# Routing and gathering the first 128 tokens during the second 128's Fourier map, with the norm's weights moved into the router and tiles placed 128 bytes over multiples of 256

## The chip, the cores and the metric

The kernel runs on one core of one Trainium2 chip. The metric is the device time of one execution in microseconds (us); the runs of the kernel before gave a median of 1440.93 us. TensorE is called PE here (PEld is its loading of stationary operands), VectorE is DVE, ScalarE is ACT, GpSimd is POOL and SyncE is SP.

## What is computed

A two-layer encoder on 256 tokens of width 1024, all in float32. Layer 0 is a retention mixer and a dense SwiGLU; layer 1 is a 2-D Fourier mixer with a linear map and a top-2-of-8 expert SwiGLU. The part that the change touches:

```python
h = h + fourier_mixer(rms_norm(h, mix_norm[1]), fnet_w_out)     # real part of a 2-D FFT, then @ w_out
t = rms_norm(h, ffn_norm[1])
logits = t @ w_router                                           # 256 x 8
top_val, top_idx = lax.top_k(logits, 2)
gates = sum(one_hot(top_idx) * softmax(top_val)[..., None])
for e in range(8):
    out = out + gates[:, e:e+1] * ((silu(t @ w_gate[e]) * (t @ w_up[e])) @ w_down[e])
h = rms_norm(h + out, final_norm)
```

Each expert has w_gate and w_up of 1024 x 3584 and w_down of 3584 x 1024.

## The kernel before

The 256 tokens are two chunks of 128, called c = 0 and 1. Every float32 operand is split into a high part, rounded to float32r by ACT (L252, weights L130), and the remainder, by DVE (L253, weights L131); a product is three matmuls (hi*hi, lo*hi, hi*lo: L247, L248, L249). Weights come as 1 MB tiles `raw` over SP's DMA queue (L104), in the order of use, into slots that are given out as soon as a tile is split; the split tiles `whi` and `wlo` have three buffers. Late in the program four more slots are lent (L905 to L909); the first of them, `y`, lies where the pool `pt` of the Fourier stage lay.

The order of work on each engine is the order in which the program is written (a manual schedule); engines meet by semaphores.

`close` (L318) ends a stage that adds to the residual X: for each of the four quarters (chunk c, half hf of the width) it does twelve 512-column matmuls, then `gained` (DVE adds the result into X, L265, and multiplies by the norm's weights into `gx`, L266), and then hands the quarter before to `sink`. For the Fourier map the sink is `r_sink` (L808): PE transposes the gained quarter (L811), ACT copies it to `xt` (L812), the high and low parts `nh`, `nl` are made and the squares are summed (L280). One quarter later the router's matmuls run, 8 columns wide and in plain float32, four of them (8 PE instructions) for each quarter (`r_mm`, L769).

`route(c)` (L774) finds the two largest logits with DVE (L777 to L783) and makes `mask`. `po` counts with PE how many tokens before this one chose each expert (L824 for chunk 0; L827 and L828 for chunk 1), DVE copies it to `pos` (L826, L829). `gates` (L785) works the weights of the two experts out on POOL.

For experts 0 and 1, `choose` (L839) makes one-hot matrices `pm` from pos and mask (L844, one for each chunk and expert), `gather` (L848) picks the tokens with 256-column matmuls (L854 with `nh`, L855 with `nl`; eight for each of four pairs of 128 columns, 32 in all), and the result is split into `xe`. `place` transposes `pm` (L866) and picks the gates (L871). In the kernel before, all this comes after both chunks are routed, and `place` comes in the middle of the first expert's first product, after one weight tile. Each weight tile of an expert is twelve 512-column matmuls; an expert has 7 blocks of six tiles.

`Aligned` places every tile of 512 bytes or more at a multiple of `ALIGN` bytes from the start of its pool. The pools begin 128 bytes over a multiple of 256 (X lies at byte 1152 of each partition), except `pt`, which is filled so that it begins at a multiple of 256. With steps of 128, tiles lie at either. The program's own addresses are: `whi`, `wlo`, `raw`, `nhi`, `nlo`, `th`, `yh`, `yl` and the experts' `hth`, `htl` 128 over a multiple of 256; the dense SwiGLU's `hth`, `htl` (178944, 183040 and on) and `tdh`, `tdl` at multiples of 256. The dense `hth` and `htl` are stationary operands of the down product, as `yh` and `yl` are of the Fourier map and the experts' `hth` and `htl` of theirs, all with `whi` or `wlo` as the moving operand.

Of the kernel before, what the change touches and what calls it, by code (L numbers as in the profile page):

```python
# [12 lines left out]
OP = mybir.AluOpType  # L13
# [8 lines left out]
NE = 8  # L22
# [18 lines left out]
class Aligned:  # L41


    ALIGN = 128

    def __init__(self, pool):
        self.pool, self.at, self.seen = pool, 0, set()
# [104 lines left out]
def body(nc, tc, a, out, upto=None):  # L152
    with ExitStack() as ctx:
# [75 lines left out]

        def route_consts(rw):  # L230
            nc.scalar.dma_start(rw, a["moe_router"][0].rearrange("(k p) e -> p k e", p=P))
            kw = dict(base=0, allow_small_or_imprecise_dtypes=True)
            ge.iota(iota8, pattern=[[1, NE]], channel_multiplier=0, **kw)
            ge.iota(slot, pattern=[[1, P]], channel_multiplier=0, **kw)
            ge.memset(ones, 1.0)
# [39 lines left out]
        def sq_tile():  # L275
            return const.tile([P, 2, 2], F32, name="sq", bufs=2)
# [38 lines left out]
                    mm3(accs[2 * c + hf], lh[j][:, cp(c)], ll[j][:, cp(c)], it[0][:, j, HALF[hf]],  # L315
                        it[1][:, j, HALF[hf]], first and j == 0, last and j == 1)

        def close(its, accs, sink, early=None):  # L318

            left = None
            for c in range(2):
                for hf in range(2):
                    for i, (it, lh, ll) in enumerate(its):
                        out_mm(accs, it, lh, ll, c, False, i == len(its) - 1, (hf,))
                    xg = gained(c, hf, accs)
                    if early:
                        early(c, hf)  # L330
                    if left:
                        sink(*left)
                    left = (c, hf, xg)
            return lambda: sink(*left)
# [269 lines left out]
        td = [pt.tile([P, 2, 512], F32R, name=n) for n in ("tdh", "tdl")]  # L604
        ts_ = [pt.tile([P, 2, 2 * H1], F32R, name=n) for n in ("tsh", "tsl")]
        rw = pt.tile([P, 8, NE], F32, name="rw")
        pt.fill(96)
        with tc.tile_pool(name="pb", bufs=1) as pb:
            pb = Aligned(pb)
# [86 lines left out]
        if upto == "B":  # L696
            return finish()


        with tc.tile_pool(name="pc", bufs=1) as pc:  # L700
            pc = Aligned(pc)
# [60 lines left out]

            xt = [pc.tile([P, 8, P], F32, name="xt", tag="fh", bufs=2) for _ in range(2)]
            lgp = [mm("lg") for _ in range(2)]
            sq, late = sq_tile(), []

            def r_mm(c, hf):
                for k in range(4 * hf, 4 * hf + 4):
# [39 lines left out]
            def r_sink(c, hf, xg):  # L808
                p = tr()
                for k in range(4):  # L810
                    te.transpose(p[:, cp(k)], xg[:, cp(k)], ident)  # L811
                se.copy(xt[c][:, 4 * hf:4 * hf + 4], p.rearrange("p (k t) -> p k t", k=4))  # L812
                for ch in late:
                    r_mm(*ch)
                late[:] = [(c, hf)]
                split(nh[:, c, HALF[hf]], nl[:, c, HALF[hf]], xg)
                square(sq, c, hf)

            left = close(its, accs, r_sink)
            po = mm("po")  # L820
            route(0)
            left()
            r_mm(1, 1)
            te.matmul(po[:, 0:8], upper, mask[:, 0], start=True, stop=True)  # L824
            route(1)
            ve.tensor_copy(pos[:, 0], po[:, :8])  # L826
            te.matmul(po[:, 8:16], ones, mask[:, 0], start=True, stop=False)  # L827
            te.matmul(po[:, 8:16], upper, mask[:, 1], start=False, stop=True)  # L828
            ve.tensor_copy(pos[:, 1], po[:, 8:16])  # L829
            gates()  # L830

        pt_.close()
        if upto == "C":
# [2 lines left out]

        with tc.tile_pool(name="pe", bufs=1) as pe:
            pe = Aligned(pe)
            def choose(e0):  # L839

                pm = pe.tile([P, 2, 2 * P], F32R, name="pm")
                for c in range(2):
                    for j in range(2):
                        ve.tensor_scalar(pm[:, c, cp(j)], slot, pos[:, c, e0 + j:e0 + j + 1],  # L844
                                         mask[:, c, e0 + j:e0 + j + 1], op0=OP.is_equal, op1=OP.mult)
                return pm

            def gather(pm, xe, q, o=None):  # L848

                o = o or mm("ga")  # L850
                for i in range(2):
                    ds = cp(2 * q + i)
                    for c in range(2):
                        te.matmul(o[:, i * 256:(i + 1) * 256], nh[:, c, ds], pm[:, c], start=c == 0, stop=False)  # L854
                        te.matmul(o[:, i * 256:(i + 1) * 256], nl[:, c, ds], pm[:, c], start=False, stop=c == 1)  # L855
                ov = o.rearrange("p (i j s) -> p j i s", i=2, j=2)
                split(xe[:, :, 0, 2 * q:2 * q + 2], xe[:, :, 1, 2 * q:2 * q + 2], ov)

            def place(pm):

                pt = pe.tile([P, 2, S], F32R, name="pt", bufs=2)
                gl = pe.tile([P, 2, NE + 1], F32, name="gl", bufs=2)
                p = tr()
                for j in range(2):
                    for c in range(2):
                        te.transpose(p[:, j * S + c * P:j * S + (c + 1) * P], pm[:, c, cp(j)].bitcast(F32), ident)  # L866
                se.copy(pt, p.rearrange("p (j t) -> p j t", j=2))
                p = acc(3)
                for j in range(2):
                    for c in range(2):  # L870
                        te.matmul(p[:, 16 * j:16 * j + NE + 1], pm[:, c, cp(j)].bitcast(F32), gts[:, c],  # L871
                                  start=c == 0, stop=c == 1)
                ve.tensor_copy(gl, p[:, :32].rearrange("p (j e) -> p j e", j=2)[:, :, :NE + 1])
                return pt, gl

            XE, PT, GT, RS = {}, {}, {}, {}

            def prep(e0):

                st = {}  # L880

                def first():
                    st["pm"] = choose(e0)
                    st["xe"] = pe.tile([P, 2, 2, 8, P], F32R, name="xe", bufs=2)
                    for j in range(2):
                        XE[e0 + j] = st["xe"][:, j]
                yield first
                for q in range(4):
                    yield lambda q=q: gather(st["pm"], st["xe"], q, acc(q) if not e0 else None)

                def last():
                    pt, gl = place(st["pm"])
                    for j in range(2):
                        PT[e0 + j] = pt[:, j]
                        GT[e0 + j] = gl[:, j, e0 + j:e0 + j + 1]
                        RS[e0 + j] = gl[:, j, NE:]
                yield last

            work = list(prep(0))
            for f in work[:-1]:  # L900
                f()
            work = work[-1:]

            i0 = W.next
            W.lend(pe.tile([P, 2048], F32, name="lent", tag="y"), i0 + 40)  # L905
# [152 lines left out]
            for u in range(NU):  # L1058
                e, b = divmod(u, 7)
                if b == 0 and e % 2 == 1 and e + 1 < NE:  # L1060
                    work += list(prep(e + 1))
                if b == 1 and e:
                    work[:0] = [lambda e=e, c=c: add_back(e - 1, c) for c in range(2)]
                if u == OVER_AT + 3:
                    work += [lambda hf=hf: final_gain(hf) for hf in range(2)]
                if u == NU - 5:
                    work += [lambda c=c: final_parts(c) for c in range(2)]
                for s, o in enumerate(moe_h(e)):
                    if s == 0 and u:
                        hidden_t(u - 1)  # L1070
                    if s == 0 and not u:
                        work.pop(0)()
                hm = pe.tile([P, 512], F32, name="hm")
                se.activation(hm, o, AF.Silu, scale=RS[e])
                for s, o in enumerate(moe_h(e)):
                    if s == 0 and work:
                        work.pop(0)()
                ve.scalar_tensor_tensor(hm, o, RS[e], hm, op0=OP.mult, op1=OP.mult)
                hms[u] = hm
                if u == NU - 1:  # L1080
                    final_start(1)
                if u:
                    moe_down(u - 1, (lambda: hidden_t(NU - 1)) if u == NU - 1 else None)
                if work:
                    work.pop(0)()
                if u == NU - 2:
                    final_start(0)
                if u == OVER_AT - 2:
                    counts()
                if u == OVER_AT - 1:  # L1090
                    most = nc.values_load(cmi[0:1, 0:1])
                    tc.mark_branch_hint_location("over", most > P, engines=[te.engine, ve.engine, nc.sync.engine])
                if u == OVER_AT:
                    nc.scalar.dma_start(gb[:1], a["final_norm"].rearrange("(o d) -> o d", o=1))
                    ov = overflow_tiles()
                    with tc.If(most > P, label="over"):  # L1096
                        overflow(**ov)
# [73 lines left out]
```

## Time and profile before

| | before |
|---|---|
| median of 3 runs | 1440.93 us (1440.27 to 1440.96) |
| the profiled execution | 1440.99 us, span 1439.2 us |
| PE busy | 1419.8 us (99%) |
| DVE, ACT, POOL busy | 1184.3, 971.0, 61.4 us |
| closing quarters of the Fourier map | about 426 to 439 us of the span |
| routing, gathering, first expert's first tiles | 439 to 457 us |
| experts | 452.6 to about 1430 us |

A row of the timeline gives start, duration, engine, line, operation, output and inputs, shape and count; a bracket at its end is the engine's idle time before it and what ended it. Matmuls overlap their neighbours, so their rate is read from start to start, not from their durations.

### The profile page before, as it was taken

Reading aid. Unit: us, or ns where it says so; the run is one execution under the profiler, and the core shown is the slowest. Engines: PE = TensorE matmul, PEld = TensorE weight load, DVE = VectorE, ACT = ScalarE, POOL = GpSimd, SP = SyncE. Lnnn points to the kernel's source line nnn. Section 1 sums busy time; section 2 is a strip of 40 time slices with the busy share of each in tenths; the row PEclk is TensorE's granted clock in tenths of the full one; section 3 lists DMA queues with packets and bytes.
Section 4 is the critical chain, followed back from the end, with each engine's and each line's share of the span. In section 5 each row is a group of like instructions: output and inputs, shape, how many; then the busy total and the mean of one; then the engine's idle time right before and its main releaser. Section 6 shows DMA issues by size and latency. Waiting matters only on the chain. (4 is left out here: it accounts for less than half of the span.)

```text
span 1439.2 us, 17455 instructions
## 1 busy us (share of the span) xinstructions
PE 1419.8 (99%) x6603; PEld 1178.0 (82%) x6603; DVE 1184.3 (82%) x1236; ACT 971.0 (67%) x1123; POOL 61.4 (4%) x95
## 2 busy tenths in 40 slices
PE   8999999999999999999999999999999999999997
PEld 6888878888888888888888888888878888888886
DVE  6876666545577999989999998998989899999996
ACT  5544446444456777777777777777777777777875
POOL 8400000000001000000000000000000000000000
PEclk9999999999999999999999999999999999999999
DMA  8646539655536989999999999999999999999980
GB/s 286 213 152 204 189 120 389 232 192 188 176 133 239 392 299 365 346 343 334 374 354 373 377 344 339 366 375 335 348 388 346 340 364 366 374 366 375 355 319 30
DMA packets 185101, 431.70 MB, mean 300 GB/s; under 512 B 7977, under 2 KB 10801, under 8 KB 185010
## 3 DMA queue, kind: packets, MB, share of 16 engines
q1 hardware_dynamic: 181424, 426.27, 82.2%
q10 hardware_dynamic: 3586, 4.24, 0.9%
q8 instruction: 54, 0.88, 0.3%
q14 instruction: 37, 0.30, 0.1%
HBM read 429.44 MB, written 1.05 MB: 299 GB/s over the span
## 5 line engine op out<-in xcount | busy, mean ns | idle before, releaser
L131 DVE TENSOR_TENSOR wlo<-raw,whi 128x1024 fp32r<-128x1024 f32 (+1 forms) x789 | 923.9, 1221 | 141.0 <-ACT whi L130 135.5
L130 ACT CAST whi<-raw 128x1024 fp32r<-128x1024 f32 (+1 forms) x789 | 786.1, 1047 | 200.7 <-PE acc L249 101.4
L247 PE MATMUL mm<-whi,xe 128*128 128x512 f32 x896 | 355.0, 396 | 0.3 <-PEq L1096 0.3
L249 PE MATMUL mm<-whi,xe 128*128 128x512 f32 x896 | 349.6, 390 | 0.0
L248 PE MATMUL mm<-wlo,xe 128*128 128x512 f32 x896 | 349.2, 390 | 0.0
L247 PE MATMUL acc<-whi,hth 128*128 128x512 f32 x528 | 206.2, 390 | 0.0
L249 PE MATMUL acc<-whi,htl 128*128 128x512 f32 x528 | 205.9, 390 | 0.0
L248 PE MATMUL acc<-wlo,hth 128*128 128x512 f32 x528 | 205.9, 390 | 0.0
L249 PEld LDWEIGHTS mm<-whi,xe 128*128 128x128 f32 x896 | 168.2, 188 | 36.0
L247 PEld LDWEIGHTS mm<-whi,xe 128*128 128x128 f32 x896 | 168.3, 188 | 34.9 <-issue 2.2
L248 PEld LDWEIGHTS mm<-wlo,xe 128*128 128x128 f32 x896 | 168.6, 188 | 32.9
L247 PE MATMUL mm<-whi,nhi 128*128 128x512 f32 (+1 forms) x352 | 135.7, 386 | 0.0
L249 PE MATMUL mm<-whi,nlo 128*128 128x512 f32 (+1 forms) x352 | 133.9, 380 | 0.0
L248 PE MATMUL mm<-wlo,nhi 128*128 128x512 f32 (+1 forms) x352 | 133.7, 380 | 0.0
L249 PEld LDWEIGHTS acc<-whi,htl 128*128 128x128 f32 x528 | 99.1, 188 | 21.1
L247 PEld LDWEIGHTS acc<-whi,hth 128*128 128x128 f32 x528 | 99.2, 188 | 20.8
L248 PEld LDWEIGHTS acc<-wlo,hth 128*128 128x128 f32 x528 | 99.2, 188 | 20.8
L252 ACT CAST hth<-tr 128x512 fp32r<-128x512 f32 (+1 forms) x67 | 38.9, 581 | 90.6 <-PE tr L293 90.6
L249 PEld LDWEIGHTS mm<-whi,nlo 128*128 128x128 f32 x352 | 66.2, 188 | 12.9
L248 PEld LDWEIGHTS mm<-wlo,nhi 128*128 128x128 f32 x352 | 66.3, 188 | 12.0
L247 PEld LDWEIGHTS mm<-whi,nhi 128*128 128x128 f32 x352 | 66.2, 188 | 11.8
L253 DVE TENSOR_TENSOR htl<-tr,hth 128x512 fp32r<-128x512 f32 (+1 forms) x67 | 45.8, 683 | 32.7 <-ACT hth L252 32.6
(279 smaller groups left out, 1037.6 us busy)
## 6 DMA issues: line engine op xcount, KB each, us to landing
raw<-in_moe_w_gate SPq DMA_DIRECT2D x110, 1024.0 KB, 7.1
raw<-in_moe_w_down SPq DMA_DIRECT2D x108, 1024.0 KB, 7.0
raw<-in_moe_w_up SPq DMA_DIRECT2D x105, 1024.0 KB, 7.1
raw<-in_ret_w_in SPq DMA_DIRECT2D x23, 1024.0 KB, 5.2
raw<-in_dense_w_gate SPq DMA_DIRECT2D x11, 1024.0 KB, 5.1
raw<-in_dense_w_up SPq DMA_DIRECT2D x11, 1024.0 KB, 8.8
raw<-in_dense_w_down SPq DMA_DIRECT2D x11, 1024.0 KB, 5.8
raw<-in_ret_w_out SPq DMA_DIRECT2D x8, 1024.0 KB, 4.8
```

What stands on the lines that cost most here:

```text
L130: self.nc.scalar.copy(hi[sl], t[sl])
L131: self.nc.vector.tensor_sub(lo[sl], t[sl], hi[sl].bitcast(F32))
L247: te.matmul(o, lh, rh, start=first, stop=False)
L248: te.matmul(o, lh, rl, start=False, stop=False)
L249: te.matmul(o, ll, rh, start=False, stop=last)
L252: se.copy(hi, src)
L253: ve.tensor_sub(lo, src, hi.bitcast(F32))
```

## The change

`ALIGN` becomes 256, so that every large tile lies 128 bytes over a multiple of 256. The norm's weights are loaded as a 128 x 8 tile `rg` and multiplied into the router's weights `rw` on POOL, so that the router can read X itself: the transposes of `r_sink` take X in place of the gained tile. `close` gets a hook `mid`: the sink of the quarter before now comes after the first six matmuls of a quarter, not after all twelve, and in the last quarter the router's matmuls for chunk 0 and `route(0)` come there too. After the quarters, chunk 0's counts, choice and gathering are done while chunk 1's last quarter, its router matmuls and its routing go on; the gathers of chunk 0 start the four accumulators `acc` and those of chunk 1 finish them. `place` comes before the first expert. The choice matrix of experts 0 and 1 lies in the buffer of `tdh` in the pool `pt`.

```diff
 class Aligned:
-    ALIGN = 128
+    ALIGN = 256
...
         def route_consts(rw):
             nc.scalar.dma_start(rw, a["moe_router"][0].rearrange("(k p) e -> p k e", p=P))
+            nc.scalar.dma_start(rg, a["ffn_norm"][1].rearrange("(k p) -> p k", p=P))
+            ge.tensor_mul(rw, rw, rg[:, :, None].to_broadcast([P, 8, NE]))
...
-        def close(its, accs, sink, early=None):
+        def close(its, accs, sink, early=None, mid=None):
...
                     for i, (it, lh, ll) in enumerate(its):
                         out_mm(accs, it, lh, ll, c, False, i == len(its) - 1, (hf,))
+                        if mid and left and not i:
+                            mid(c, hf)
+                            sink(*left)
                     xg = gained(c, hf, accs)
                     if early:
                         early(c, hf)
-                    if left:
+                    if left and not mid:
                         sink(*left)
...
+        def choose(pm, e0, c):
+            for j in range(2):
+                ve.tensor_scalar(pm[:, c, cp(j)], slot, pos[:, c, e0 + j:e0 + j + 1],
+                                 mask[:, c, e0 + j:e0 + j + 1], op0=OP.is_equal, op1=OP.mult)
+
+        def gather(o, pm, q, c):
+            for i in range(2):
+                ds = cp(2 * q + i)
+                te.matmul(o[:, i * 256:(i + 1) * 256], nh[:, c, ds], pm[:, c], start=not c and not i, stop=False)
+                te.matmul(o[:, i * 256:(i + 1) * 256], nl[:, c, ds], pm[:, c], start=False, stop=bool(c and i))
...
             def r_sink(c, hf, xg):
                 p = tr()
                 for k in range(4):
-                    te.transpose(p[:, cp(k)], xg[:, cp(k)], ident)
+                    te.transpose(p[:, cp(k)], X[:, c, cp(4 * hf + k)], ident)
                 se.copy(xt[c][:, 4 * hf:4 * hf + 4], p.rearrange("p (k t) -> p k t", k=4))
-                for ch in late:
-                    r_mm(*ch)
-                late[:] = [(c, hf)]
                 split(nh[:, c, HALF[hf]], nl[:, c, HALF[hf]], xg)
                 square(sq, c, hf)
 
-            left = close(its, accs, r_sink)
-            po = mm("po")
-            route(0)
+            def r_mid(c, hf):
+                if (c, hf) == (1, 1):
+                    r_mm(0, 0)
+                    r_mm(0, 1)
+                    route(0)
+
+            left = close(its, accs, r_sink, mid=r_mid)
+            po, pm = mm("po"), pt.tile([P, 2, 2 * P], F32R, name="pm0", tag="tdh")
+            te.matmul(po[:, 0:8], upper, mask[:, 0], start=True, stop=True)
+            r_mm(1, 0)
+            ve.tensor_copy(pos[:, 0], po[:, :8])
+            choose(pm, 0, 0)
             left()
+            go = [acc(q) for q in range(4)]
+            for q in range(2):
+                gather(go[q], pm, q, 0)
             r_mm(1, 1)
-            te.matmul(po[:, 0:8], upper, mask[:, 0], start=True, stop=True)
             route(1)
-            ve.tensor_copy(pos[:, 0], po[:, :8])
-            te.matmul(po[:, 8:16], ones, mask[:, 0], start=True, stop=False)
-            te.matmul(po[:, 8:16], upper, mask[:, 1], start=False, stop=True)
-            ve.tensor_copy(pos[:, 1], po[:, 8:16])
+            for q in range(2, 4):
+                gather(go[q], pm, q, 0)
+            po = tr()
+            te.matmul(po[:, 0:8], ones, mask[:, 0], start=True, stop=False)
+            te.matmul(po[:, 0:8], upper, mask[:, 1], start=False, stop=True)
+            ve.tensor_copy(pos[:, 1], po[:, :8])
+            choose(pm, 0, 1)
             gates()
+            for q in range(4):
+                gather(go[q], pm, q, 1)
+            ro = place(pm)
...
-            work = list(prep(0))
-            for f in work[:-1]:
+            for f in prep(0, go, ro):
                 f()
-            work = work[-1:]
+            work = []
...
                     if s == 0 and u:
                         hidden_t(u - 1)
-                    if s == 0 and not u:
-                        work.pop(0)()
```

`prep(0, go, ro)` only splits what was gathered (`split_xe`) and copies what `place` left in PSUM (`placed`); for the later pairs of experts `prep` does what it did.

## Rows read from the trace of the kernel before

**Rows 1.** Page, busy time of the engines over the span.
```profile
PE 1419.8 (99%) x6603; PEld 1178.0 (82%) x6603; DVE 1184.3 (82%) x1236; ACT 971.0 (67%) x1123; POOL 61.4 (4%) x95
```

**Rows 2.** Busy time by stretch of the span; the first row names the columns.
```profile
core 0: us, PE busy (x) PEld busy (x) DVE busy (x) ACT busy (x) POOL busy (x), PEclk, DMA share, GB/s
...
439.20:444.10 4.90, 3.90 (x35) 3.75 (x33) 4.30 (x16) 3.45 (x8) 0.57 (x3) 1.00 0.00 0
444.20:450.90 6.70, 5.11 (x23) 5.04 (x24) 2.49 (x10) 0.86 (x2) 4.41 (x15) 0.50 0.55 184
460.00:1400.00 940.00, 939.70 (x4303) 777.85 (x4303) 864.88 (x835) 726.73 (x794) 0.00 (x0) 1.00 0.98 357
```

**Rows 3.** Timeline of PE from the last closing quarter to the first gather.
```profile
439.13 0.60 PE L811 MATMUL tr<-ident,gx 128*128 128x128 f32 x4
...
440.88 0.63 PE L811 MATMUL tr<-ident,gx 128*128 128x128 f32 x4 [0.36 <-ACT nhi L252]
...
441.35 1.90 PE L769 MATMUL lg<-rw,xt 128*128 128x8 f32 x16
...
444.89 0.59 PE L827 MATMUL po<-mask,ones 128*128 128x8 f32 x2 [1.43 <-DVE pos L826]
...
446.81 0.55 PE L854 MATMUL acc<-pm,nhi 128*128 128x256 f32 x1 [0.90 <-DVE pm L844]
```

**Rows 4.** Timeline of DVE, chunk 0's routing, then chunk 1's position and choice.
```profile
441.50 0.16 DVE L777 COPY lgt<-lg 128x8 f32<-128x8 f32 x1
...
442.65 0.23 DVE L783 SCALAR_TENSOR_TENSOR mask<-iota,if,o 128x8 f32<-128x8 f32 x1
...
445.95 0.17 DVE L829 COPY pos<-po 128x8 f32<-128x8 f32 x1 [1.11 <-PE po L828]
446.06 1.11 DVE L844 TENSOR_SCALAR pm<-slot,pos,mask 128x128 fp32r<-128x128 f32 x4
```

**Rows 5.** Timeline of PE: 20th of 32 gathers, first and second expert tiles.
```profile
451.01 0.28 PE L855 MATMUL acc<-pm,nlo 128*128 128x256 f32 x1
...
452.56 0.40 PE L247 MATMUL mm<-whi,xe 128*128 128x512 f32 x1
...
456.56 0.48 PE L247 MATMUL mm<-whi,xe 128*128 128x512 f32 x1
```

**Rows 6.** Timeline of ACT and DVE: the first expert weight tiles split after the gathers.
```profile
453.24 3.89 ACT L130 CAST whi<-raw 128x1024 fp32r<-128x1024 f32 x4
...
454.32 4.63 DVE L131 TENSOR_TENSOR wlo<-raw,whi 128x1024 fp32r<-128x1024 f32 x4 [0.26 <-ACT whi L130]
```

**Rows 7.** Timeline of PE: dense closing (47 matmuls), then the Fourier map (71).
```profile
390.80 0.39 PE L248 MATMUL acc<-wlo,hth 128*128 128x512 f32 x1
...
401.50 0.40 PE L249 MATMUL acc<-whi,htl 128*128 128x512 f32 x1
...
415.75 0.40 PE L248 MATMUL acc<-wlo,yh 128*128 128x512 f32 x1
...
431.63 0.39 PE L249 MATMUL acc<-whi,yl 128*128 128x512 f32 x1
```

**Rows 8.** Groups of PE from 250 to 401.6 us; L248, L249 have x88 each too.
```profile
L247 PE MATMUL acc<-whi,hth 128*128 128x512 f32 x88 | 34.9, 397 | 0.0
```

**Rows 9.** Timeline of DVE: the first closing quarter's result added into X.
```profile
429.98 0.68 DVE L265 TENSOR_TENSOR X<-X,acc 128x512 f32<-128x512 f32 x1
```

**Rows 10.** Waits from 460 to 1400 us: us in total, times, longest.
```profile
SPq L104 <- DVE wlo L131: 774.3, 313, 9.9
...
DVE wlo L131 <- DMA raw<-in_moe_w_down: 1.3, 5, 0.3
```

**Rows 11.** Timeline of SP's queue: the first lent slots.
```profile
446.07 0.92 SPq L104 DMA_DIRECT2D lent<-in_moe_w_up  x2
```

**Rows 12.** Timeline of ACT where the router's weights are loaded.
```profile
226.51 0.45 ACTq L231 DMA_DIRECT2D rw<-in_moe_router  x1
...
236.76 2.00 ACT L130 CAST whi<-raw 128x1024 fp32r<-128x1024 f32 x2 [3.43 <-PE mm L249]
```

More of the change, by code (lines that the diff above doesn't have):

```diff
@@ L606, in body @@
         rw = pt.tile([P, 8, NE], F32, name="rw")
+        rg = pt.tile([P, 8], F32, name="rg")
         pt.fill(96)
@@ L697, in body, with place @@
             return finish()
+        def choose(pm, e0, c):
[7 more added lines that the diff above has]
+                te.matmul(o[:, i * 256:(i + 1) * 256], nl[:, c, ds], pm[:, c], start=False, stop=bool(c and i))
+        def place(pm):
+            p = tr()
+            for j in range(2):
+                for c in range(2):
+                    te.transpose(p[:, j * S + c * P:j * S + (c + 1) * P], pm[:, c, cp(j)].bitcast(F32), ident)
+            g = mm("gl")
+            for j in range(2):
+                for c in range(2):
+                    te.matmul(g[:, 16 * j:16 * j + NE + 1], pm[:, c, cp(j)].bitcast(F32), gts[:, c],
+                              start=c == 0, stop=c == 1)
+            return p, g
         with tc.tile_pool(name="pc", bufs=1) as pc:
@@ L764, in body @@
             lgp = [mm("lg") for _ in range(2)]
-            sq, late = sq_tile(), []
+            sq = sq_tile()
             def r_mm(c, hf):
@@ L838, in body, with split_xe @@
             pe = Aligned(pe)
[L839 to L855, printed above, removed]
+            def split_xe(o, xe, q):
@@ L856, in gather, with placed @@
                 ov = o.rearrange("p (i j s) -> p j i s", i=2, j=2)
                 split(xe[:, :, 0, 2 * q:2 * q + 2], xe[:, :, 1, 2 * q:2 * q + 2], ov)
-            def place(pm):
+            def placed(o):
                 pt = pe.tile([P, 2, S], F32R, name="pt", bufs=2)
                 gl = pe.tile([P, 2, NE + 1], F32, name="gl", bufs=2)
[L863 to L873, printed above, removed]
+                se.copy(pt, o[0].rearrange("p (j t) -> p j t", j=2))
+                ve.tensor_copy(gl, o[1][:, :32].rearrange("p (j e) -> p j e", j=2)[:, :, :NE + 1])
@@ L874, in place, with prep @@
                 return pt, gl
             XE, PT, GT, RS = {}, {}, {}, {}
-            def prep(e0):
+            def prep(e0, go=None, ro=None):
                 st = {}
                 def first():
-                    st["pm"] = choose(e0)
+                    if not go:
+                        st["pm"] = pe.tile([P, 2, 2 * P], F32R, name="pm")
+                        for c in range(2):
+                            choose(st["pm"], e0, c)
                     st["xe"] = pe.tile([P, 2, 2, 8, P], F32R, name="xe", bufs=2)
@@ L887, in prep, with part @@
                 yield first
+                def part(q):
+                    o = go[q] if go else mm("ga")
+                    for c in () if go else range(2):
+                        gather(o, st["pm"], q, c)
+                    split_xe(o, st["xe"], q)
                 for q in range(4):
-                    yield lambda q=q: gather(st["pm"], st["xe"], q, acc(q) if not e0 else None)
+                    yield lambda q=q: part(q)
                 def last():
-                    pt, gl = place(st["pm"])
+                    pt, gl = placed(ro or place(st["pm"]))
                     for j in range(2):
```

## The prediction

> **What bounds the kernel now.** I read the busy times first. PE is busy for 1419.8 of 1439.2 us [rows 1], so only two things can move the end: PE time that is lost around the change, and the rate at which PE's matmuls follow each other. Then the stretches: among the experts PE is busy 939.7 of 940 us at the full clock, while from 439.2 to 450.9 us it is idle for 2.6 us in all, and from 444.2 to 450.9 us the granted clock is 0.50, that is 1.2 instead of 2.4 GHz [rows 2]. So the routing is the soft place. Its timeline shows what PE waits for: 0.36 us for `nhi` before the last transposes, 1.43 us for chunk 0's `pos` (which stands behind chunk 1's routing on DVE), and 0.90 us for the choice [rows 3]. After that PE gathers: 32 matmuls from 446.81 to 452.56 us, the first 19 in 4.20 us, the other 13 in 1.55 us [rows 3, 5], so 221 ns each and then 119 ns each. At the later rate the 32 take 3.81 us; the half clock costs 1.94 us here. Losses before: 0.36 + 1.43 + 0.90 + 1.94 = 4.6 us, without the count matmuls that ran at half clock too.
>
> **The reordering.** The number of PE instructions stays: as many transposes, router matmuls, counts and gathers, and `place` only goes ahead of the first expert tile. So I compare PE's losses. Where it will wait in the new order:
>
> - The sink after six matmuls. The transposes of quarter 0 now need X's sum, which DVE has ready at 429.98 + 0.68 = 430.66 us [rows 9]; six matmuls of the second quarter end their slots at 431.63 - 5 x 0.227 = 430.50 us [rows 7]. 0.2 us; DVE's part of the sink then delays the next sum a little. For the four quarters 0.3 us.
> - Before chunk 0's gathers. After the last matmul (0.39 us till its result) DVE must do the sum, the gained product of the same width (0.68 each), chunk 0's pos (0.17) and two of four choices (0.55) [rows 4, 9]: 2.5 us, and about 0.4 more because `route(0)` and one split stand ahead of the sum on DVE. In that time PE has the counts, eight router instructions (half of 1.90 us) and four transposes (0.63) [rows 3], together with 0.3 for the counts 1.9 us. Without the choice PE stands for 1.0 us; I take 1.3 with the signals.
> - Before chunk 1's counts. `route(1)` takes 441.50 to 442.88 us on chunk 0's rows, 1.38 us [rows 4], and PE has eight gathers (0.95) and the first counts under it. 0.4 us.
> - Before chunk 1's gathers. Counts, pos, choice as now, where that wait was 0.90 us [rows 3]. 1.0 us.
>
> Sum 3.0 us against 4.6 us: a gain of 1.6 us, if PE keeps the full clock. What is late next is the split of the second expert tile. Now it is needed at 456.56 us; its casts begin at 453.24 and the first `wlo` comes 1.16 us (a quarter of 4.63) after 454.32, at 455.48 us [rows 5, 6]. In the new order `place` is done before the experts begin, and PE wants that tile at 456.56 - 1.6 = 455.0 us, while ACT must first copy what `place` left, and its casts begin hardly earlier. That ties; 0 to 0.3 us, I take 0.1. The gain is 1.5 us, between 1.2 and 1.9.
>
> **The clock.** This is what the gain hangs on. Before, the last dense matmuls end and the transposes begin at 439.13 us, and the next dense work is the first gather at 446.81 us: 7.7 us of transposes, 8-column matmuls and waiting, within which the clock fell [rows 2, 3]. In the new order the quarter's last six matmuls come after `route(0)`'s matmuls, and the longest such stretch before the gathers is about 3 us; then come eight gathers, one us without, eight more, and about 2 us without. No row shows what the clock does after a gap of that kind; I take the shorter gaps as a reason to expect 2.4 GHz, at little better than even.
>
> The Trainium skill, "TensorE: Matmul & The Clock Gate", Part 1, speaks against that: the throttled clock is the default state and activity releases it. By that rule thin gathers between waits could leave PE at 1.2 GHz; the trace agrees so far, since the clock fell in just this work. The sum by it is the second rival's.
>
> **The 256-byte steps.** The 47 dense matmuls with `hth` or `htl` as stationary operand take 10.70 us for 46 steps, 232.6 ns each; the 71 with `yh` or `yl` take 15.88 us for 70 steps, 226.9 ns, at the same clock, shape and moving operands [rows 7]. The first tiles lie at a multiple of 256, the second 128 over. There are 3 x 88 = 264 dense ones [rows 8]: 264 x 5.7 ns = 1.5 us. If the place is not the cause, nothing is gained; if the fastest steps seen are reached, some 1.6. I take 1.5, as it is the only difference that the listing of the tiles shows, and as PE does not wait there. `whi`, `wlo` and `raw` keep their place, so the experts' rate stays.
>
> **The norm in the router.** One more load from ACT's queue and a product on POOL. The load of `rw` takes 0.45 us to issue [rows 12]; if ACT also waits for a semaphore of an older load, the idle 3.43 us before 236.76 us [rows 12] takes that up. POOL is busy 61.4 us in all [rows 1], and the product is needed 200 us later. Nothing; without that cover at most 3.4 us of PE waiting, which the end would see.
>
> **Transfers.** The first lent slot `y` reaches into the pool `pt`. Now it is issued at 446.07 us [rows 11]; in the new order `pm0` lies in `pt` until `place` has read it, at about 452.3 us, and everything behind it in SP's queue waits, four lent loads and the refills. 6.2 us later at most. The cover is the lead of the loads: among the experts the queue waits 774 us for free slots, and DVE waits 1.3 us for weights [rows 10]. With 15 slots of 2.72 us each (twelve matmuls), weights are there tens of us ahead. I take nothing.
>
> **Sum.** The profiled execution took 1440.99 us, 0.06 above the median of the runs. 1440.99 - 1.5 - 1.5 = 1438.0 us.
>
> **The rivals.**
>
> - Clock holds, both gains come: 1438.0 us, from 1437.0 to 1438.8 by the bounds above. Chance 0.50.
> - The clock falls as before and returns as before, at about 451 us. Then half of chunk 0's gathers, the router's and count matmuls and the first of chunk 1's gathers run at half clock: some 16 gathers x 0.1 us and 0.3 for the rest, 1.9 us, mostly on the chain, which eats the routing's gain. 1439.6 us. For it: the thin work; against it: the shorter gaps. Chance 0.20.
> - The same, but gathers in two thin groups do not bring the clock back before the experts: chunk 1's 13 other gathers 1.3 us more and `place` about as much again. 1441 to 1442 us. Chance 0.11.
> - The clock holds and the steps of 256 do nothing: 1439.5 us. Chance 0.08.
> - Slower: the late transfers. Should the lead be under 6 us anywhere, PE waits for what is missing, up to 6.2 us: 1444.2 us with both gains. For it: DMA is busy 0.98 of the time among the experts [rows 2], so what is lost is not won back; against it: the waits for slots. It decides from a lead of 6.2 us down. Chance 0.05.
> - The change does more: other tiles whose place changes (the Fourier tables, `pm0`) speed their matmuls as well, and the waits overlap better than I allow. 1436.6 us. Chance 0.06.
>
> **How the numbers follow.** 0.2% of the median, about what a measurement of this kernel can tell from no change, is 2.9 us: faster ends at 1438.05 us, slower begins at 1443.8 us. The likeliest case lies on that bound; a little over half of it, 0.28, and the last case, 0.06, are faster, and 0.02 for a clock that falls late: 0.36. Slower is the transfers' case and 0.01 beside it: 0.06. The rest, 0.58, is within 0.2%. The range for 8 in 10 goes from 1436.8 us to 1441.2 us; it leaves out the transfers, half of the third case and part of the last. The likeliest case's own range is 1437.0 to 1438.8.
>
> **What would show it.** Granted clock 1.00 from 439 to 453 us, gathers about 119 ns apart in three groups, and PE waits of about 0.3, 1.3, 0.4 and 1.0 us; the dense down product at 227 ns; the second expert tile begun some 3 us earlier than at 456.56 us; the first `lent` load at about 452 us and still no PE wait among the experts. The prediction is wrong if the clock falls to 0.50 in the gathers, if the dense steps stay at 232 ns, or if PE waits for `raw` anywhere.

## The result, and the profile after

The kernel after takes 1451.93 us (median of 6 runs, 1450.66 to 1452.35), the kernel before 1440.85 us in the same comparison (6 runs, 1440.27 to 1440.99). The ratio is 1.0073, 95% interval 1.0062 to 1.0084: slower by 11 us, where 3 us less had been forecast. The profiled execution of the kernel after took 1450.66 us with a span of 1448.9 us, 9.7 us longer than that of before; the rows below account for these 9.7 us.

**The largest loss lies 200 us ahead of the routing, in the dense SwiGLU.** First ACT's timeline with its DMA issues (ACTq), where the router's weights are loaded:

```profile
225.04 0.39 ACTq L660 DMA_DIRECT2D tabr<-in_dft_s  x1
...
226.50 0.45 ACTq L232 DMA_DIRECT2D rw<-in_moe_router  x1
226.99 5.32 ACTq L233 DMA_DIRECT2D rg<-in_ffn_norm  x1
232.41 1.27 ACT L667 ACTIVATE gs<-mm,rs 128x512 f32<-128x512 f32 x2 [6.66 <-issue]
```

`rw` is issued in 0.45 us as before [rows 12]; `rg`, right behind it, takes 5.32 us, and ACT stands still for it. What ACT does next is the silu `gs`, which reads PE's accumulators `mm` and so sets when PE may write them again. PE's timeline there:

```profile
228.17 0.39 PE L252 MATMUL mm<-whi,nlo 128*128 128x512 f32 x1
233.15 0.80 PE L250 MATMUL mm<-whi,nhi 128*128 128x512 f32 x1 [4.59 <-ACT gs L667]
233.75 0.63 PE L251 MATMUL mm<-wlo,nhi 128*128 128x512 f32 x1
...
238.44 0.54 PE L250 MATMUL mm<-whi,nhi 128*128 128x512 f32 x1
238.82 0.40 PE L251 MATMUL mm<-wlo,nhi 128*128 128x512 f32 x1
```

PE idles for 4.59 us, and the next matmul starts 4.98 us after the one before, 4.75 more than the usual 0.23. Then 13 matmuls take 238.82 - 233.15 = 5.67 us in place of 13 x 0.227 = 2.95: half clock, 2.7 us more. Together 7.5 us.

**The 256-byte steps do what was forecast.** The end of the dense closing on PE, 47 matmuls as in [rows 7]:

```profile
397.05 0.40 PE L251 MATMUL acc<-wlo,hth 128*128 128x512 f32 x1
...
407.52 0.39 PE L252 MATMUL acc<-whi,htl 128*128 128x512 f32 x1
```

10.47 us for 46 steps, 227.6 ns each in place of 232.6. The last one starts 6.02 us after that of before (401.50 us, [rows 7]): the 7.5 us have become 6.0.

**The routing loses 3.7 us more.** The stretches, with the columns of [rows 2]:

```profile
231.90:238.70 6.80, 5.55 (x13) 4.39 (x14) 2.36 (x2) 3.16 (x5) 0.00 (x0) 0.50 1.07 377
...
450.40:460.60 10.20, 9.30 (x46) 9.21 (x45) 2.20 (x11) 0.13 (x2) 5.28 (x17) 0.50 0.01 2
...
470.00:1400.00 930.00, 929.70 (x4257) 769.57 (x4256) 856.75 (x827) 718.95 (x785) 0.00 (x0) 1.00 0.99 360
```

The clock is at 0.50 (1.2 GHz) for 10.2 us of the routing, where it was for 6.7 us before [rows 2]; among the experts PE is as full as ever. PE's timeline there, to be read against [rows 3, 5]:

```profile
449.55 0.39 PE L717 MATMUL acc<-pm,nhi 128*128 128x256 f32 x1 [0.79 <-DVE pm L710]
449.77 0.28 PE L718 MATMUL acc<-pm,nlo 128*128 128x256 f32 x1
449.89 0.28 PE L717 MATMUL acc<-pm,nhi 128*128 128x256 f32 x1
...
455.95 0.58 PE L717 MATMUL acc<-pm,nhi 128*128 128x256 f32 x1 [0.90 <-DVE pm L710]
456.33 0.42 PE L718 MATMUL acc<-pm,nlo 128*128 128x256 f32 x1
...
459.31 0.41 PE L718 MATMUL acc<-pm,nlo 128*128 128x256 f32 x1
...
462.26 0.50 PE L250 MATMUL mm<-whi,xe 128*128 128x512 f32 x1 [0.81 <-ACT xe L255]
...
466.42 0.50 PE L251 MATMUL mm<-wlo,xe 128*128 128x512 f32 x1 [0.65 <-DVE wlo L132]
466.76 0.40 PE L252 MATMUL mm<-whi,xe 128*128 128x512 f32 x1
```

The first gathers start 120 ns apart, but all of chunk 1's are 213 ns apart, (459.31 - 456.33) / 14. The first expert matmul comes at 462.26 us, 9.7 us after that of before [rows 5]. That is not yet like for like: `place` is done by then, and in the kernel before it came only behind the first tile and took 456.56 - 455.31 = 1.25 us. But here PE waits twice more, for `xe` and for `wlo`, and at the third matmul of the second tile, with `place` behind it in both kernels, it is again 9.7 us late (466.76 against 457.10 us). PE in the kernel before:

```profile
455.31 0.60 PE L866 MATMUL tr<-ident,pm 128*128 128x128 f32 x4
...
457.10 0.39 PE L249 MATMUL mm<-whi,xe 128*128 128x512 f32 x1
```

ACT's first cast into `xe` and SP's first lent load say why PE waits there:

```profile
461.62 2.06 ACT L255 CAST xe<-acc 128x512 fp32r<-128x512 f32 x4 [11.09 <-PE gl L729]
...
461.60 0.92 SPq L105 DMA_DIRECT2D lent<-in_moe_w_up  x2
```

Both start when the last matmul of `place` (L729) is done, although the gathers that `xe` copies ended two us earlier. `xe` lies in the pool that is opened when `pc` and `pt` are closed, and `pm0`, in `pt`, has its last reader in `place`. The late lent load itself costs nothing. Waits from 470 to 1400 us, in total, times and longest:

```profile
SPq L105 <- DVE wlo L132: 772.0, 314, 9.9
...
DVE wlo L132 <- DMA raw<-in_moe_w_down: 1.3, 5, 0.3
```

That is as before [rows 10]. So the 9.7 us are 7.5 (the load of `rg`) - 1.5 (steps of 256) + 3.7 (routing). The experiments test each of the three and take the last one apart.

### The profile page after: what moved, and what is told of

It reads as the page before. It is cut to its first block, busy times and chain, and to the rows that moved or that the text cites. A ratio compares the mean times of both kernels' runs of the same rounds, so it can differ in the third digit from the quotient of the medians.

```text
span 1448.9 us, 17452 instructions
## 1 busy us (share of the span) xinstructions
PE 1424.0 (98%) x6603; PEld 1181.0 (82%) x6603; DVE 1183.8 (82%) x1236; ACT 970.5 (67%) x1123; POOL 61.9 (4%) x96
```

## The experiments

Twelve kernels ran. Where a ratio is given it is against the kernel before, run on the same chip in between.

**The load of `rg` moved (a1_rg_later).** In the kernel after, load and product go to a later block of the dense stage.

```diff
-            nc.scalar.dma_start(rg, ...)          # behind rw
-            ge.tensor_mul(rw, rw, rg...)
+                if u == 2:                        # two blocks later
+                    nc.scalar.dma_start(rg, ...)
+                    ge.tensor_mul(rw, rw, rg...)
```

> The changed kernel with the load of rg and its product moved from the first to the third block of the dense SwiGLU, some 60 us later, when the loads issued beside it have landed. Theory (the queue is full): the 5.32 us issue of rg is ACT waiting for room behind the small loads issued just before it; later the issue takes about 0.45 us like that of rw, PE's 4.6 us wait at 228 us and the half clock after it go, and the time falls by the 7.5 us that PE lost there, to 1444.4 us. Rival (the elements): 4-byte elements take 5.3 us to issue wherever it is done; ACT stands as long in the later block, PE waits there too for a part of it, and the time stays above 1447 us.

1443.17 us (1439.4 to 1445.03, 10 runs), ratio 1.0005 [0.9995, 1.0015]. `rg` is issued in 0.38 us at 276.9 us, PE no longer waits for `gs`, and all of the 7.5 us are gone: the last dense matmul starts at 400.08 us in place of 407.52. The times fall in two groups, 4 of 10 between 1439.4 and 1440.2 and 6 between 1442.6 and 1445.0, with a mean granted clock of 0.998 to 0.999 in the first and 0.994 to 0.996 in the second. The profiled run, 1443.76 us, is of the second; two of its stretches, columns as above:

```profile
442.60:452.80 10.20, 9.30 (x46) 9.21 (x45) 2.57 (x11) 0.49 (x2) 5.26 (x17) 0.50 0.01 2
...
456.30:459.60 3.30, 3.30 (x9) 2.54 (x8) 2.98 (x5) 3.30 (x5) 0.00 (x0) 0.50 1.04 406
```

The clock falls in the gathers, comes back, and falls again among the first expert matmuls, behind the wait for `xe`.

**The load of `rg` alone (a2_rg_in_before).** The kernel before with the load, its result unread.

```diff
             nc.scalar.dma_start(rw, ...)
+            nc.scalar.dma_start(rg, a["ffn_norm"][1].rearrange("(k p) -> p k", p=P))
```

> The kernel before with the load of rg alone added, in the place that the change gives it, and not used. If the load's issue is what costs the dense stage its time, this alone costs 7.5 us: 1448.4 us, with an ACT gap of 6.7 us at 226 us and the clock at 0.50 from about 232 us. Rival: it takes the other edits as well (the steps of 256 or the product on POOL); then 1440.9 us.

1448.58 us (1447.99 to 1450.47, 4 runs) beside 1441.29 us for the kernel before, ratio 1.0053 [1.0037, 1.0068]. The issue takes 5.35 us, PE waits 4.6 us for `gs`, the clock is at 0.50 from 232.3 to 239.0 us: 7.3 us from one DMA that nobody waits for.

**The steps of 256 alone (a3_step_256).** The kernel before with one line changed.

```diff
-    ALIGN = 128
+    ALIGN = 256
```

> The kernel before with ALIGN 256 alone. Theory: the 264 dense down matmuls go from 232.6 to 227 ns, 1.5 us: 1439.4 us. Rival: the slower rate came from what else ran in the dense stage, and the gain of the changed kernel there is chance: 1440.9 us and 232 ns.

1439.89 us (1439.04 to 1441.63, 11 runs), ratio 0.9990 [0.9981, 0.9999]. The last dense matmul on PE's timeline starts 1.45 us before that of [rows 7]:

```profile
400.05 0.39 PE L249 MATMUL acc<-whi,htl 128*128 128x512 f32 x1
```

**Why the issue takes 5.3 us.** Five kernels asked this. A piece is one unbroken run of bytes of a load: `rw` has 1024 of 32 bytes, `rg` 1024 of 4. In a4_rg_first the two loads change places in the kernel after (the product is as it was).

```diff
+            nc.scalar.dma_start(rg, ...)
             nc.scalar.dma_start(rw, ...)
-            nc.scalar.dma_start(rg, ...)
```

> The changed kernel with the loads of rg and rw in the opposite order; nothing else. Queue theory: whichever comes last stands, so rg takes about 0.45 us to issue and rw some 5 us, and the time is that of the changed kernel, 1451.9 us. Rival (the elements of 4 bytes): rg still takes 5 us and rw 0.45 us.

1451.06 us, one run.

```profile
226.33 0.45 ACTq L232 DMA_DIRECT2D rg<-in_ffn_norm  x1
...
226.81 5.41 ACTq L233 DMA_DIRECT2D rw<-in_moe_router  x1
```

Now `rg` is issued in 0.45 us and `rw` takes 5.41 us: it is the place in the queue, not the tile. Then the size of what comes second. In c2_few and c3_half the kernel before loads 8 pieces of 32 bytes, or 512 of 4 bytes, behind `rw`, unread.

```diff
             nc.scalar.dma_start(rw, ...)
+            nc.scalar.dma_start(rg[:8], a["ffn_norm"][1, 0:64].rearrange("(k p) -> k p", p=8))     # c2_few
+            nc.scalar.dma_start(rg[:64], a["ffn_norm"][1, 0:512].rearrange("(k p) -> p k", p=64))  # c3_half
```

> The kernel before with an unread load of 8 pieces of 32 bytes right behind the load of rw, on ACT's queue. Theory (the count of pieces in the queue holds the issue up): issued in about 0.4 us, time as before, 1440.9 us. Rival (any load issued right behind rw waits until rw has drained): some 5.3 us again and 1448.5 us.

> The kernel before with an unread load of 512 pieces of 4 bytes right behind the load of rw, on ACT's queue: half of the norm's weights. Theory (the issue waits until the queue has room for its pieces, and pieces drain at about 170 for each us): 512 / 170 = 3.0 us less than with 1024, an issue of about 2.3 us, which the 3.4 us of ACT's idle time nearly cover, so 1441 to 1442 us. Rival (one fixed wait for the queue to be empty): 5.3 us and 1448.5 us.

1449.03 and 1448.33 us, one run each. The kernel after had 1024 pieces in the 5.8 us from the issue of `rw` to the end of that of `rg`, about the 170 for each us that c3_half reckoned with. But my theory of the count falls: 8 pieces wait as long as 512 or 1024 do, as the rivals had it. And what they wait for is not that `rw` is through: `rw` lands 16.2 us after its issue in d1_few_first and 17.0 us in c1_rg_pool. ACT's queue in c2_few, and the landing of `tabr` from its issue (min/median/max):

```profile
224.90 0.39 ACTq L654 DMA_DIRECT2D tabr<-in_dft_s  x1
...
226.85 5.34 ACTq L232 DMA_DIRECT2D rg<-in_ffn_norm  x1
```

```profile
DMA to landing us min/median/max: 7.0/7.0/7.0
```

`tabr` lands at 224.90 + 7.0 = 231.9 us, and the issue ends at 226.85 + 5.34 = 232.19. In the kernel after it is 225.04 + 7.1 = 232.1 and 232.31, and in the other three with a long issue the distance is 0.1 to 0.3 us too. So in all five kernels the issue ends just after the oldest of the four loads ahead is in. A fixed time fits as well, since `tabr` is issued 1.5 us ahead of the first load of 1024 pieces in each of them: from that load's issue to the end of the long one it is 5.8 to 5.9 us in all five. No run tells these two apart. Beside that, it is open what makes a load wait at all: the queue takes four loads and the fifth waits; or whatever stands behind a load of 1024 pieces waits until these have found room. d1_few_first puts the 8 pieces ahead of `rw`, so that `rw` is the fifth.

```diff
+            nc.scalar.dma_start(rg[:8], a["ffn_norm"][1, 0:64].rearrange("(k p) -> k p", p=8))
             nc.scalar.dma_start(rw, ...)
```

> The kernel before with the unread load of 8 pieces of 32 bytes ahead of the load of rw, so that rw's 1024 pieces are the fifth load of ACT's queue within 2 us. Theory (what is issued behind a load of 1024 pieces waits until these have found room, and that is when tabr lands): rw is issued in about 0.45 us, nothing waits behind it, 1441 us. Rival (the queue takes four loads, and the fifth waits until the first of them, tabr, has landed, however large it is): rw's issue takes some 5.3 us and the time is 1448.5 us.

1440.85 us, one run. ACT's timeline:

```profile
226.52 0.35 ACTq L231 DMA_DIRECT2D rg<-in_ffn_norm  x1
226.91 0.40 ACTq L232 DMA_DIRECT2D rw<-in_moe_router  x1
227.41 1.26 ACT L661 ACTIVATE gs<-mm,rs 128x512 f32<-128x512 f32 x2 [1.64 <-POOL ones L236]
```

The fifth load is issued in 0.40 us. It is not the number of loads; it is standing behind the 1024 pieces. In the kernel before `rw` was the last of its group and nothing stood behind it on ACT's queue until 404.6 us.

In c1_rg_pool the load stays where it is in the kernel after, but goes out from POOL, in two halves.

```diff
-            nc.scalar.dma_start(rg, ...)
+            for k0 in (0, 4):
+                nc.gpsimd.dma_start(rg[:, k0:k0 + 4], a["ffn_norm"][1, k0 * P:(k0 + 4) * P].rearrange("(k p) -> p k", p=P))
```

> The kernel after with the load of rg at its old place, but issued from POOL's queue, as two halves of 512 pieces of 4 bytes. Theory (ACT's own queue is full behind the 1024 pieces of rw): ACT issues rw in about 0.45 us and goes on to the silu; PE does not wait for gs; dense stage as before, so 1439.5 us or 1443.5 us, by what the clock does in the routing. Rival (the 16 DMA engines are full, whichever queue asks): ACT or POOL stands some 5 us and ACT's silu is late again if it is ACT; 1451 us.

1441.79 us, one run, between the two times named: the clock fell twice, for 3.4 us each. ACT and POOL in the timeline:

```profile
226.72 1.02 POOL L234 DMA_DIRECT2D rg<-in_ffn_norm  x1
227.19 1.27 ACT L668 ACTIVATE gs<-mm,rs 128x512 f32<-128x512 f32 x2 [1.30 <-POOL rs L290]
...
233.04 0.77 POOL L234 DMA_DIRECT2D rg<-in_ffn_norm  x1 [5.31 <-issue]
```

ACT goes on at once. POOL stands for 5.31 us between its two halves, as the rival had it for one of the two engines; it costs nothing, as nobody waits for POOL here. The second half goes out 0.3 to 0.5 us after the first has landed (5.8 to 6.0 us from its issue), so POOL may only have waited for its own first half. That the DMA engines were full whichever queue asks is not so: in the kernel after, SP issued a weight load in 0.37 us in the middle of ACT's 5.32 us.

```profile
228.45 0.37 SPq L105 DMA_DIRECT2D raw<-in_dense_w_gate  x1
```

The Trainium skill, "DMA: Bandwidth & Descriptors", section "Issuing engines are not separate DMA queues", says that issuing from several engines saves only the sequencer's time to initiate a DMA, and that this is usually small relative to the DMA itself. That ACT is spared this time agrees with this run; small it was not, 5.32 us of the 23.8 us from the issue of `rg` to its landing in the kernel after.

**The choice matrix out of `pt` (b1_pm_in_whi).** On top of a1, `pm0` lies in a buffer of the weights' high parts, so that no pool that closes has a late reader.

```diff
-            po, pm = mm("po"), pt.tile([P, 2, 2 * P], F32R, name="pm0", tag="tdh")
+            po, pm = mm("po"), hilo.tile([P, 2, D], F32R, name="whi")[:, :, :2 * P]
```

> The kernel after with the late norm load, and with the choice matrix of experts 0 and 1 in a buffer of the weights' high parts in place of the buffer of tdh. Theory (the pool of the choice matrix holds back the tiles that lie over it): ACT's first cast into xe starts before the last matmul of place, PE's waits of 0.81 and 0.65 us at the first expert's first two tiles go, the first lent load is issued before 455 us, and the span is about 1.4 us shorter than with the late load alone at the same clock: about 1441.5 us where the clock falls, 1438 us where it holds. Rival (those waits are ACT's and DVE's backlog, whatever the buffer): xe starts no earlier against place, and the time is that of the late load alone, 1443.2 us.

1437.43 us (1437.19 to 1441.01, 7 runs), ratio 0.9982 [0.9971, 0.9993]; 4 runs lie at 1437.2 to 1437.4, the others at 1439.2 to 1441.0 with a lower mean clock. Against the two groups of a1 the gain is 2.4 and 3.0 us, where 1.4 was expected. ACT's first cast into `xe` and the first lent load:

```profile
447.76 2.05 ACT L253 CAST xe<-acc 128x512 fp32r<-128x512 f32 x4 [4.65 <-PE acc L719]
...
446.16 0.92 SPq L105 DMA_DIRECT2D lent<-in_moe_w_up  x2
```

The cast follows a gather now, and PE's waits at the first two expert tiles are gone. In this profile the clock is 1.00 throughout, so it shows the new order undisturbed. PE's waits in it:

```profile
442.13 0.38 PE L718 MATMUL acc<-whi,nhi 128*128 128x256 f32 x1 [0.79 <-DVE whi L711]
...
445.61 0.39 PE L873 MATMUL tr<-mask,upper 128*128 128x8 f32 x2 [0.30 <-DVE mask L818]
446.89 0.39 PE L718 MATMUL acc<-whi,nhi 128*128 128x256 f32 x1 [0.90 <-DVE whi L711]
```

(`whi` names the choice matrix here.) 0.79, 0.30 and 0.90 us, where I had put 1.3, 0.4 and 1.0.

**The waits filled (b2_busy, b3_both).** Ten matmuls of 512 columns whose results nobody reads stand in PE's three waits; b2 is a1 with them, b3 is b1 with them.

```diff
+            def busy(o, n):
+                for _ in range(n):
+                    te.matmul(o, nh[:, 0, :P], nh[:, 0, HALF[0]], start=True, stop=True)
...
+            busy(go[3], 4)        # before chunk 0's gathers
...
+            busy(tr(), 2)         # before chunk 1's counts
...
+            busy(mm("busy"), 4)   # behind choose(pm, 0, 1)
```

> The kernel after with the late norm load, and with ten matmuls of 512 columns whose results nobody reads, in PE's three waits: four before chunk 0's gathers, two before chunk 1's counts, four after chunk 1's choice. They take 2.2 us at full clock if the waits don't hide them. Theory (the half clock after thin work is what the new order loses): the granted clock is 1.00 from 439 us to the experts, gathers are about 120 ns apart, all runs are in one group, and the median is 1439 to 1440.5 us. Rival (the waits themselves and the order cost the time, the clock little): the clock is higher but the median stays at 1443 us or rises by up to 2 us.

> Late norm load, choice matrix in a buffer of the weights' high parts, and the ten unread matmuls. Theory (the norm load, the clock and the tiles behind the choice matrix are all that the change loses): 1437 to 1438.5 us, as was predicted for the change itself. Rival (the new order has a cost of its own): not below 1439.5 us, the time of before with steps of 256 alone.

b2: 1440.0 us (1439.78 to 1440.88, 10 runs), ratio 0.9992 [0.9983, 1.0001]. b3: 1437.63 us (1437.21 to 1438.34, 9 runs), ratio 0.9975 [0.9966, 0.9985]. The second group of times is gone in both. The routing of b3 by stretch:

```profile
439.00:444.00 5.00, 4.88 (x38) 4.41 (x38) 3.51 (x8) 2.33 (x6) 0.96 (x3) 1.00 0.00 0
444.00:450.00 6.00, 5.94 (x45) 5.12 (x43) 3.46 (x13) 2.26 (x5) 4.17 (x15) 1.00 0.45 137
```

The work that nobody reads takes no time of its own: b3's span, 1435.4 us, equals that of b1 where the clock held. What it buys is the clock in every run (a mean of 0.998 to 0.999 in all 19). The gap between b2 and b3, 2.4 us, is the price of `pm0` in `pt`.

**The same in the old order (b4_before_busy).** The kernel before with steps of 256 and ten such matmuls in its own two waits; no reordering.

```diff
+            busy(acc(0), 6)       # behind the counts of chunk 0
             route(1)
...
+            busy(acc(1), 4)
             gates()
```

> The kernel before with steps of 256 and with ten unread matmuls of 512 columns in its routing: six before chunk 0's pos is ready and four before the gates; no other part of the change. Theory (half clock is worth some 2 us there, and matmuls in the waits hold the clock): clock 1.00 from 446 us on, 19 gathers of the first kind at about 120 ns in place of 221, 1437.5 to 1438.5 us, so that the reordering is not needed for the gain. Rival (the clock was already lost before those matmuls run and needs a longer stretch to come back, or the matmuls delay the chain): 1439.9 us or above.

1438.58 us (1437.43 to 1440.19, 11 runs), ratio 0.9980 [0.9971, 0.9989]. The same stretch of the span in a3_step_256 and then in this kernel:

```profile
443.80:450.50 6.70, 5.79 (x27) 5.72 (x28) 2.63 (x7) 1.17 (x2) 3.61 (x12) 0.50 0.74 256
```

```profile
443.80:450.50 6.70, 6.70 (x45) 5.95 (x46) 3.86 (x9) 2.93 (x5) 3.68 (x12) 1.00 0.76 269
```

45 matmuls, four of them unread, in place of 27 in the same time, and a span of 1435.7 us in place of 1438.1. Here the clock is not held in every run (5 of 11 lie at 1437.4 to 1437.5 with a mean of 0.998 to 0.999, the others at 1438.6 to 1440.2 with 0.996 to 0.997). Where it is, the old order is as fast as the new one to 0.3 us.

## Why the prediction was wrong

**The step that failed is the norm in the router.** It was costed at nothing, with 3.4 us at most. The reason given was ACT's idle time of 3.43 us before 236.76 us [rows 12]. That a wait of ACT for an older load was conceivable stood in the sentence; what failed is the cover. ACT's idle time from 233.3 to 236.8 us covers nothing that stands right behind the load at 227 us, and that was the silu, which frees PE's accumulators. PE went on 0.74 us after `gs` began (233.15 - 232.41) and would have gone on at 228.40 us, so ACT had to be free by 227.66 us. The issue of `rw` ended at 226.96 us [rows 12]: 0.7 us of room, not 3.4. The bound also left out the clock: 2.7 of the 7.5 us are the 13 matmuls at half clock behind the wait. a2 shows the whole cost without the rest of the change, a1 takes it away, c1 takes it away by another queue.

**The clock: the third rival, with a later fall.** I gave the full clock a little better than even, and the third rival 0.11. In the profile of the kernel after it falls at 450.4 us, among chunk 0's gathers, and stays at 0.50 to 460.6 us: through chunk 1's gathers and `place`, as the third rival said. The Trainium skill, "TensorE: Matmul & The Clock Gate", Part 1, cited there as speaking against the full clock, has it that activity releases a clock that is throttled by default; the runs agree, as ten matmuls in the waits held it in all runs of b2 and b3, and ten in the old order's in 5 of 11 (b4). What I had not seen is that one kernel can go both ways: a1 and b1 ran with the full clock and without it. Its price is the distance of the two groups, from the groups' middles 1443.82 - 1439.67 = 4.1 us in a1 and 1440.84 - 1437.28 = 3.6 us in b1; the third rival's 1441 to 1442 us, against 1438.0, had put it at 3 to 4. That the half clock is what parts the groups rests on the mean clock of each run and on the filled waits of b2 and b3.

**The tie of the second expert tile** was put at 0.1 us. Here the step missed that `pm0` keeps `pt` alive until `place` is done, and that `xe` lies over it; I had seen this for the lent loads and not for `xe`. It costs 2.4 us (b2 against b3): 1.5 us are the waits of 0.81 and 0.65 us, and slower matmuls around them are most of the rest.

**What held.** PE's waits in the new order, 2.0 us without those inside the quarters against 2.7 forecast for the same three. The gain of the order at full clock: b3 is 2.7 us shorter in span than a3, against 1.5 forecast, both with the end of the old order's half clock in them; but b3 has the ten unread matmuls, which the change has not. The steps of 256: 227.6 ns forecast as 226.9, 1.45 us against 1.5. The transfers: nothing, as said. With the three losses removed the change gives 1437.63 us (b3), where 1438.0 was forecast for the change itself.

**What the reordering is worth by itself** is little: where the clock holds, b4 without it comes within 0.3 us of b1 and b3. The half clock was one part of the 4.6 us of losses, and it can be taken away without moving anything; the waits of the old order (0.36 + 1.43 + 0.90 = 2.7 us, [rows 3]) then cost little more than those of the new one (2.0 us and what the quarters lose).

**What stays open.** What a load behind 1024 pieces waits for: the runs show that it ends with the landing of `tabr`, or 5.8 to 5.9 us after the first such load, in five kernels, and exclude the number of loads, the size of the one that waits, and a stop for every queue. No run shortened `tabr` or moved it alone. Why the clock falls in some runs of a1, b1 and b4 and not in others was not settled either; the profiles show that it did. And the median of the kernel after lies 1.3 us above its profiled run, which no profile covers.

## What to carry to other kernels

A DMA issue is an instruction of the engine that issues it, and it can take microseconds: ask what that engine does next and who waits for that, and take as cover only idle time ahead of that next step. Put a load of many small pieces last in its group, or on the queue of an engine that nobody waits for; and a tile borrowed from a pool that is about to close makes its last reader a barrier for all that lies over it. Where thin work between dense stretches lets TensorE's clock fall, a few unread matmuls in the waits can be worth as much as a new order of the work.

## What the runs showed of the hardware that was not expected

- A load of 8 pieces of 32 bytes took 5.34 us to issue behind one of 1024 pieces on ACT's queue, and 0.35 us ahead of it (c2_few, d1_few_first). `rg`'s 1024 pieces behind the same load took 5.32 us (kernel after), 512 took 5.31 us (c3_half).
- One idle stretch of PE of 4.6 us was followed by 13 matmuls of 512 columns at half clock, although PE ran without a gap from 233.15 us on; 0.50 was granted from 231.9, while PE still stood, until 238.7 us (kernel after).
- Stationary operands at multiples of 256 bytes, with moving operands 128 bytes over, made the dense down product's 128x512 matmuls follow each other every 232.6 ns; 128 bytes over as well, every 227.6 ns (kernel before; a3_step_256 and kernel after).
